# One 512-column matmul in place of two pieces of 264 and 248 in the projections of a two-block network on Trainium2

## The chip, the cores and the metric

The kernel runs on one core of one Trainium2 chip. The metric is the device time of one execution in microseconds (us). Three runs of the kernel before gave 1912.60, 1915.05 and 1916.12 us, a median of 1915.05 us.

## What is computed

One sequence of 512 tokens with 1024 features goes through two blocks, all in float32.

```
for l in range(2):                         # block 1, over 528 rows: 16 meta tokens + 512
    a, g, zc, q, k, v, za, qi, ki, wi = split(h @ w_in[l])
    y_conv = silu(layer_norm(conv31(a * sigmoid(g)))) * silu(zc)
    y_attn = attention(q, k, v, keys = top 132 by relu(qi.ki)*wi) * silu(za)
    h = layer_norm(alpha * h + [y_conv, y_attn] @ w_out[l])
# block 2, over the 512 tokens
proj = rmsnorm(h) @ w_in_2                 # windowed attention, gated linear attention, gates
merged = sigmoid(g_att) * (attn @ w_branch_attn) + sigmoid(g_gla) * (gla @ w_branch_gla)
h = h + merged @ w_out_2
h = h + expert_choice_ffn(rmsnorm(h))      # 16 experts, 64 tokens each
h = h + sigmoid(rmsnorm(h) @ w_ple_gate) * (p @ w_ple);  out = rmsnorm(h)
```

## The kernel before, in words

**Projections.** Nearly all products of activations with weights go through `proj` (L166 to L183). The result is feature-major: 128 output features on the partitions, tokens along the columns. The 1024 input features are eight tiles of 128 (`KT`). Weights and activations are each split in a high and a low part of type float32r (`wh`, `wl`; `hTh`, `hTl` or `xTh`, `xTl`), and three products per tile are added up in PSUM: high by high, high weight by low activation, low weight by high activation. One output tile is thus 8 x 3 products over all its tokens. In a product the 128 x 128 weights are loaded into TensorE and the activations stream through. `segs` names the tokens: either the two halves (0, 264) and (264, 528) of the 528 rows of block 1, in a PSUM bank each, or a single stretch of 512 tokens, in one bank. A stretch is walked in steps of `self.piece` columns, and each step is one matmul with a weight load of its own:

```
n = segs[0][1] - segs[0][0]
...
k = self.piece or c1 - c0
for x in range(0, n, k):
    nc.tensor.matmul(ps[:m, s, x:min(x + k, n)], a[:, t, :m], b[:, c0 + x:min(c0 + x + k, c1)],
```

**Where 512 tokens are one stretch.** In block 1: the index queries of both layers, and in the second layer also the queries, the two gates and the output projection (activations `hT`, `yah`/`yal`, `ych`/`ycl`). In block 2: every projection (activations `xT`, `at`, `yg`, `mh`/`ml`), among them one with only 48 output features.

**Weights.** `load_w` brings 256 columns of weights from HBM over SyncE's queue (SP); `split_w` makes `wh` on ScalarE (ACT, L159) and `wl` on VectorE (DVE, L160).

**Block 1.** Beside the projections, the convolution has 31 taps for four tiles of 128 channels. A tile's input `u` is made at L325 from two products; some tiles' taps go to ACT and GpSimd (POOL) and the others to DVE, first tap at L313 and thirty at L315. After all four tiles the channel statistics (L641) start the tail of the layer, which ends in the output projection. The selection of keys (L398, L399) and a pass of the softmax of the attention (L568) also run on DVE.

**Block 2 and the experts.** After the projections with their attention and linear attention comes the output projection. Then the weights of the 16 experts stream from HBM through buffers that earlier work leaves free (`rawe`, issued at L1484 and L1489 on SP), and each is multiplied as it arrives (L1505). The end is a gate product (L1587) of 512 columns with 128 x 128 weights of type float32r in each matmul, issued without pieces, and the final norm.

**The order of work.** Instructions are written in streams of different urgency (`levels`, `go`), and a scheduler puts them in an order per engine when the program is built, by urgency and by modelled durations (`schedule_with_timeline_sim=True`). Each engine executes its own list in that order. A change of the matmuls thus also changes where other instructions stand.

Of the kernel before, what the change touches and what calls it, by code (L numbers as in the profile page):

```python
# [16 lines left out]
PSUM = bass.MemoryType.PSUM  # L17
DRAM = bass.MemoryType.DRAM
# [9 lines left out]
TOPK = min(256, L // 4)  # L28
# [5 lines left out]
def constants():  # L34
# [6 lines left out]
    p = np.arange(128)[:, None]  # L41
# [5 lines left out]
    # second block  # L47
# [10 lines left out]
    same = (p // 64) == (c // 64)  # L58
# [10 lines left out]
class Net:  # L69
    def __init__(self, tc, I, out, dbg=None, upto=99):  # L70
        self.tc, self.nc, self.I, self.out, self.dbg = tc, tc.nc, I, out, dbg
        self.upto = upto
        self.bgq = []
        self.plan = [
            (('w', 'topk', 'tail', 'idx', 'proj', 'conv', 'att', 'ag', 'rest', 'fill'),
             ('ag0', 'idx', 'q', 'k', 'sc', 'v', 'ag2', 'ag3', 'topk', 'ag1', 'zc', 'att', 'za'),
             (2, 0, 1, 3),
             (2, 3, 1, 0),
             (0, 1, 2)),
            (('w', 'tail', 'idx', 'conv', 'proj', 'att', 'ag', 'topk', 'rest', 'fill'),  # L80
             ('idx', 'q', 'k', 'sc', 'ag1', 'v', 'ag0', 'ag3', 'topk', 'ag2', 'att', 'za', 'zc'),
             (2, 0, 1, 3),
             (2, 3, 1, 0),
             (0, 1)),
        ]
        self.order2 = ('w', 'crit', 'att', 'gla', 'main', 'late', 'fill')
        self.gn0, self.apull, self.gpull, self.ng = 2, 3, (1, 0, 2, 1), 0
        self.early = ("u", "szc", "cv", "qi", "v", "sm", "sm", "parts", "hw", "hl", "raw", "raw", "raw", "c1")
        self.last = ("raw", "u", "szc", "qi")
        self.cycle = ("u", "szc", "qi", "v", "sm", "sm", "hw", "hl", "raw", "raw", "raw")  # L90
        self.piece = 264
        self.swap = True
        self.stack = True
        self.sqsum, self.sqe, self.xlp = 'v', 'AAAAAAAA', ()
        self.pairs2 = False
        self.pairs, self.spare = False, None
        self.cur = None
        self.pos = 0

    def levels(self, *names):  # L100
        """streams of instructions, the earlier named the more urgent to the scheduler"""
# [11 lines left out]
    def go(self, name):  # L113
        """continue in the stream of that name"""
# [105 lines left out]
    def pair(self, out, k):  # L220
        """keys of two heads on the partitions -> side by side, each on its own half of the partitions"""
# [6 lines left out]
    def halves(self, name, q):  # L228
        """two heads of 64 on the partitions of q [128, x, n] -> high parts of the one beside the low parts of the same"""
# [8 lines left out]
    def dots(self, out, qs, p, x, kh, kl):  # L238
        """products of head (x, p) with keys, whose high parts are on both halves of the partitions"""
# [17 lines left out]
    def layer(self, l):  # L257
# [15 lines left out]
        # per-channel vectors of the convolution, channels on partitions  # L273
# [21 lines left out]
        # convolution input  # L295
# [40 lines left out]
        def p_idx():  # L336
            self.go("idx")
            # index keys and queries
# [18 lines left out]
        # index scores  # L357
# [34 lines left out]
        # selection of the TOPK largest scores of each row, as an additive bias  # L392
# [10 lines left out]
        # the same for rows hardly longer than TOPK: all but the smallest, ties to the lower index  # L403
# [68 lines left out]
        # attention  # L472
# [4 lines left out]
        def gated(col, r, src):  # L477
            """rows of the attention, turned and gated"""
# [146 lines left out]
        # layer norm over the channels of the convolution, tokens on partitions  # L625
# [45 lines left out]
        # output projection, residual and layer norm  # L671
# [70 lines left out]
    def embedding_product(self):  # L742
        """per-layer embedding product, kept in DRAM until the end"""
# [6 lines left out]
        w = []  # L750
# [21 lines left out]
    def rms(self, dst, src, gain):  # L772
        """dst = src / rms(src) * gain, rows on partitions"""
# [8 lines left out]
    def scaled(self, t, ps, raw):  # L782
        """columns times their scale, which a raw product needn't wait for"""
# [4 lines left out]
    def to_tokens(self, ps, evac, raw=False):  # L788
        """feature-major [128, 512] in PSUM -> PSUM [128 tokens, 4, 128]"""
# [48 lines left out]
    def window_attn(self, n):  # L838
        """generator of steps for the query tile n"""
# [192 lines left out]
    def second_block(self):  # L1032
# [29 lines left out]
        # last layer norm's gain and offset, and the rms norm, features on partitions  # L1062
# [38 lines left out]
        # the rows' scale joins after the products  # L1101
# [10 lines left out]
        # windowed attention inputs  # L1112
# [30 lines left out]
        # gated linear attention inputs  # L1143
# [41 lines left out]
        # gated linear attention, with projections in between  # L1185
# [41 lines left out]
        # normalised output, gated  # L1227
# [14 lines left out]
        # merged branches  # L1242
# [17 lines left out]
    def experts(self, mx):  # L1260
# [19 lines left out]
        # output projection, residual, router product and statistics  # L1280
# [44 lines left out]
        # affinities  # L1325
# [32 lines left out]
        # slots on partitions (twice), and indices along the free dimension on every partition  # L1358
# [9 lines left out]
        # expert feed-forward: the weights stream by, two rows of 128 at a time  # L1368
# [106 lines left out]
        def chunk(w, t):  # L1475
            """rows t and t + 1 of the tiles of w, each a list of pieces side by side"""
# [42 lines left out]
        # per-layer embedding gate's weights, split while the last expert is computed  # L1519
# [16 lines left out]
        # per-layer embedding and final norm, a tile of tokens at a time  # L1536
# [14 lines left out]
        def rms4():  # L1551
            """half the reciprocal root mean squares of the rows"""
# [117 lines left out]
```

## Time and profile before

| | |
|---|---|
| three runs | 1912.60, 1915.05, 1916.12 us |
| profiled execution: its time is given as its span | 1904.8 us |
| mean granted TensorE clock | 0.968 |
| PE busy (TensorE matmuls) | 1785.8 us, 94% of the span, 11679 instructions |
| PEld busy (weight loads) | 1404.4 us, 74%, 11679 instructions |
| DVE busy | 1087.8 us, 57% |
| ACT busy | 831.8 us, 44% |
| POOL busy | 226.6 us, 12% |
| HBM read | 302.60 MB |

The span reaches from the first to the last instruction; the runs' median lies 10.2 us above it. Matmuls are pipelined: the duration of one is longer than its distance from the next, so this document takes the price of a matmul from the starts of those that follow each other, and "busy" of PE is the time in which at least one is under way. In the rows, `128*128` are the rows and columns of the weights and `128x264 f32` is the matmul's output.

### The profile page before, as it was taken

What the parts mean: (1) busy time and instruction counts of PE and PEld (TensorE: products, weight loads), DVE (VectorE), ACT (ScalarE), POOL (GpSimd) and SP (SyncE); (2) the same over time, 40 slices, a digit from 0 to 9 for tenths busy, and PEclk for the clock granted to TensorE, in tenths of its full rate; (3) what the DMA queues carried; (4) which work ended last, traced back from release to release, by engine and by line L of the source; (5) the groups of instructions that cost most, each with busy time, mean ns of one, the idle gap of its engine ahead of it and who ended that gap; (6) DMA issues with size and microseconds to landing.
All of it is one profiled execution on the core that took longest, in us unless ns stands there. A gap on an engine that the chain in (4) does not pass through costs nothing.

```text
span 1904.8 us, 28702 instructions
## 1 busy us (share of the span) xinstructions
PE 1785.8 (94%) x11679; PEld 1404.4 (74%) x11679; DVE 1087.8 (57%) x2019; ACT 831.8 (44%) x1384; POOL 226.6 (12%) x154
## 2 busy tenths in 40 slices
PE   6999979889999899799999999999799999999978
PEld 6889868878988799797788899999444544344346
DVE  3889994667799976864443446544422323323254
ACT  4864656456567353633355544323122221221245
POOL 1621863000068300000000000000000000000000
PEclk9999999889999899899999999999899999999989
DMA  5213111122122122222112248456599999999961
GB/s 188 67 45 90 45 45 45 29 69 67 56 58 77 45 67 67 79 86 67 34 45 89 79 139 266 144 200 244 209 381 409 409 409 409 409 409 409 409 253 44
DMA packets 164083, 318.67 MB, mean 167 GB/s; under 512 B 12738, under 2 KB 102522, under 8 KB 163824
## 3 DMA queue, kind: packets, MB, share of 16 engines
q1 hardware_dynamic: 160832, 312.63, 45.3%
q10 hardware_dynamic: 3120, 4.21, 0.7%
q8 instruction: 92, 1.51, 0.3%
q14 instruction: 39, 0.32, 0.0%
HBM read 302.60 MB, written 14.16 MB: 166 GB/s over the span
## 4 chain that ended last, share of the span: by engine, by line
PE 74%; DVE 16%; ACT 5%; issue 3%; DMA 2%; POOL 0%; SPq 0%; ACTq 0%; DVEq 0%; POOLq 0%
PE pp L181 36%; PE pp L1505 17%; DVE cv L315 3%; PE pp L1587 2%; DVE wl L160 2%; PE pgat L1396 2%; PE psc L1449 2%; PE phid L1426 2%; PE pidx L243 1%; PE po L550 1%; DVE acc L399 1%; DVE m L398 1%; PE pidx L242 1%; PE po L889 1%; DMA rawe<-in_w_exp_up 1%
## 5 line engine op out<-in xcount | busy, mean ns | idle before, releaser
L310 POOL TENSOR_TENSOR cv<-cv,prod 128x528 f32<-128x528 f32 (+1 forms) x150 | 226.4, 1509 | 417.5 <-ACT prod L308 409.6
L159 ACT CAST wh<-raw 128x1024 fp32r<-128x1024 f32 (+2 forms) x149 | 151.0, 1016 | 257.6 <-PE pp L181 230.6
L1505 PE MATMUL pp<-rawe,xf 128*64 128x512 f32 x1024 | 246.9, 606 | 2.6 <-DMA rawe<-in_w_exp_up 1.0
L181 PE MATMUL pp<-hTh,wh 128*128 128x264 f32 (+2 forms) x1056 | 226.5, 294 | 13.5 <-ACT th L324 4.9
L160 DVE TENSOR_TENSOR wl<-raw,wh 128x1024 fp32r<-128x1024 f32 (+2 forms) x149 | 188.8, 1267 | 69.3 <-ACT wh L159 60.8
L181 PE MATMUL pp<-hTl,wh 128*128 128x264 f32 (+2 forms) x1056 | 223.6, 292 | 0.0
L181 PE MATMUL pp<-hTh,wl 128*128 128x264 f32 (+2 forms) x1056 | 223.6, 291 | 0.0
L181 PEld LDWEIGHTS pp<-hTh,wh 128*128 128x128 f32 (+1 forms) x1056 | 167.8, 192 | 23.9 <-issue 7.9
L1505 PEld LDWEIGHTS pp<-rawe,xf 128*64 128x64 f32 x1024 | 78.5, 138 | 136.2 <-issue 129.4
L181 PEld LDWEIGHTS pp<-hTl,wh 128*128 128x128 f32 (+1 forms) x1056 | 166.7, 192 | 8.5 <-issue 8.1
L181 PEld LDWEIGHTS pp<-hTh,wl 128*128 128x128 f32 (+1 forms) x1056 | 166.7, 192 | 7.9 <-issue 7.5
L181 PE MATMUL pp<-xTh,wh 128*128 128x264 f32 (+1 forms) x752 | 156.8, 290 | 2.9 <-ACT op L980 2.3
L181 PE MATMUL pp<-xTl,wh 128*128 128x264 f32 (+1 forms) x752 | 158.3, 290 | 0.4 <-DVE xTl L1075 0.4
L181 PE MATMUL pp<-xTh,wl 128*128 128x264 f32 (+1 forms) x752 | 156.4, 288 | 0.0
L308 ACT ACTIVATE prod<-u,taps 128x528 f32<-128x528 f32 (+1 forms) x150 | 107.2, 728 | 42.2 <-POOL cv L310 41.8
L181 PEld LDWEIGHTS pp<-xTh,wh 128*128 128x128 f32 (+1 forms) x752 | 116.7, 190 | 5.6 <-ACT op L980 2.5
L181 PEld LDWEIGHTS pp<-xTl,wh 128*128 128x128 f32 (+1 forms) x752 | 116.5, 190 | 3.6 <-issue 2.6
L1505 PE MATMUL pp<-rawe,hid 128*64 128x512 f32 x512 | 118.7, 593 | 0.2 <-DMA rawe<-in_w_exp_down 0.2
L181 PEld LDWEIGHTS pp<-xTh,wl 128*128 128x128 f32 (+1 forms) x752 | 116.2, 189 | 3.4 <-issue 3.3
L1428 ACT COPY hid<-phid 128x512 f32<-128x512 f32 x16 | 9.4, 586 | 204.6 <-PE phid L1426 181.6
L1505 PEld LDWEIGHTS pp<-rawe,hid 128*64 128x64 f32 x512 | 42.2, 137 | 68.8 <-issue 64.9
L315 DVE SCALAR_TENSOR_TENSOR cv<-u,taps,cv 128x512 f32<-128x512 f32 (+1 forms) x90 | 89.0, 1000 | 0.6
(505 smaller groups left out, 3171.7 us busy)
## 6 DMA issues: line engine op xcount, KB each, us to landing
rawe<-in_w_exp_down SPq DMA_DIRECT2D x54, 1024.0 KB, 15.3
rawe<-in_w_exp_up SPq DMA_DIRECT2D x52, 1024.0 KB, 15.3
rawe<-in_w_exp_gate SPq DMA_DIRECT2D x51, 1024.0 KB, 14.4
raw<-in_w_in SPq DMA_DIRECT2D x45, 1024.0 KB, 5.5
rawe<-in_w_exp_gate SPq DMA_DIRECT2D x26, 512.0 KB, 16.5
rawe<-in_w_exp_up SPq DMA_DIRECT2D x22, 512.0 KB, 16.4
raw<-in_w_in SPq DMA_DIRECT2D x20, 512.0 KB, 4.3
rawe<-in_w_exp_down SPq DMA_DIRECT2D x20, 512.0 KB, 13.0
```

The source lines that it names most:

```text
L159: nc.scalar.copy(wh, raw_view)
L160: nc.vector.tensor_sub(wl, raw_view, wh.bitcast(F32))
L181: nc.tensor.matmul(ps[:m, s, x:min(x + k, n)], a[:, t, :m], b[:, c0 + x:min(c0 + x + k, c1)], start=(t == 0 and pi == 0 and x == 0), stop= ...
L242: nc.tensor.matmul(out, qs[:, p, x, :], kh, start=True, stop=False)
L308: nc.scalar.activation(pr, src, AF.Identity, scale=taps[:, c, j:j + 1], bias=0.0 if j else cvec[:, c, 31:32])
L310: nc.gpsimd.tensor_tensor(cv[:, c, :], cv[:, c, :], pr, op=ALU.add)
L315: nc.vector.scalar_tensor_tensor(cv[:, c, :], src, taps[:, c, j:j + 1], cv[:, c, :], op0=ALU.mult, op1=ALU.add)
L1396: nc.tensor.matmul(ps, oh[:, i, :], (zh, zl)[k][:, s, i, :], start=(i == 0 and k == 0), stop=(i == 3 and k == 1))
L1426: nc.tensor.matmul(ph[:, t, :], ul[:, t * 128:(t + 1) * 128], both, start=True, stop=True)
L1449: nc.tensor.matmul(ps, ohts[j][:, 128 * i:128 * (i + 1)], Ys[j][:, k, s * 512:(s + 1) * 512], start=(k == 0), stop=(k == 1))
L1505: nc.tensor.matmul(ps[64 * k:64 * k + 64, s, :], lhs, r, start=(t == 0), stop=(t == KT - 2), skip_group_check=True)
L1587: nc.tensor.matmul(ps[k][:, k, :], a[:, t, :], wp[t][:, w, k * 512:(k + 1) * 512], start=(t == 0 and pi == 0), stop=(t == KT - 1 and pi == 2))
```

## The change

`self.piece` becomes 512, so that the loop above runs once for a stretch of 512 tokens. Stretches of 264 are as before.

```diff
         self.cycle = ("u", "szc", "qi", "v", "sm", "sm", "hw", "hl", "raw", "raw", "raw")
-        self.piece = 264
+        self.piece = 512
         self.swap = True
```

The rest of the diff blanks comments and docstrings; line numbers stay. In the program, 2280 matmuls of 264 columns and 2280 of 248 columns become 2280 of 512 columns. The matmuls of L181 in stretches of 264 (2592) remain.

The order of the instructions changes with it. On PE in block 2, in the projections of `xT` (`xTh`, `xTl`) between pieces of the windowed attention (`po` and `tp`), there stood before

```order
L181 MATMUL pp<-xTl,wh 128x264
L181 MATMUL pp<-xTl,wh 128x248
L181 MATMUL pp<-xTh,wl 128x264
L181 MATMUL pp<-xTh,wl 128x248
L889 MATMUL po<-pT,v_8051 64x512
L883 MATMUL tp<-base,sm 128x128 x8
L181 MATMUL pp<-xTh,wh 128x264
L181 MATMUL pp<-xTh,wh 128x248
L889 MATMUL po<-pT,v_8051 64x512
```

and now stands

```order
L181 MATMUL pp<-xTh,wh 128x512
L181 MATMUL pp<-xTl,wh 128x512
L889 MATMUL po<-pT,v_7379 64x512
L883 MATMUL tp<-base,sm 128x128 x6
L889 MATMUL po<-pT,v_7379 64x512
L883 MATMUL tp<-base,sm 128x128 x6
L181 MATMUL pp<-xTh,wl 128x512
```

Each pair of pieces is one row now, and the attention's pieces stand closer together here.

On DVE in the second layer of block 1, around the input `u` and the first tap (`cv<-u,taps,cvec`, L313) of the last tile of the convolution that DVE computes, there stood before

```order
L160 TENSOR_TENSOR wl<-raw,wh 128x1024
L325 SCALAR_TENSOR_TENSOR u<-th,pp 128x528
L315 SCALAR_TENSOR_TENSOR cv<-u,taps,cv 128x512
L533 TENSOR_TENSOR smm_6476<-psm,acc 128x128
L313 TENSOR_SCALAR cv<-u,taps,cvec 128x512
L315 SCALAR_TENSOR_TENSOR cv<-u,taps,cv 128x512
L534 TENSOR_REDUCE mi<-smm_6476 128x8
L315 SCALAR_TENSOR_TENSOR cv<-u,taps,cv 128x512 x3
L492 TENSOR_TENSOR yas<-po,rs 128x512
L315 SCALAR_TENSOR_TENSOR cv<-u,taps,cv 128x512 x2
L568 ISA smb,mx<-pidx,acc,mi 128x256
```

and now stands

```order
L568 ISA smb,mx<-pidx,acc,mi 128x256
L568 ISA mx 128x1
L315 SCALAR_TENSOR_TENSOR cv<-u,taps,cv 128x512
L570 TENSOR_SCALAR mx<-mx 128x2
L160 TENSOR_TENSOR wl<-raw,wh 128x1024
L315 SCALAR_TENSOR_TENSOR cv<-u,taps,cv 128x512
L579 SCALAR_TENSOR_TENSOR smm_6188<-smm_6188,mx 128x128
L325 SCALAR_TENSOR_TENSOR u<-th,pp 128x528
L315 SCALAR_TENSOR_TENSOR cv<-u,taps,cv 128x512
L313 TENSOR_SCALAR cv<-u,taps,cvec 128x512
```

The first tap of this tile stood ahead of the eight softmax steps (L568, 128x256) of a query tile, and stands behind them now, with six more taps of the other tile ahead of it.

A little later on DVE, just ahead of the channel statistics (L641) of the same layer, there stood before

```order
L579 SCALAR_TENSOR_TENSOR smm_6579<-smm_6579,mx 128x128
L160 TENSOR_TENSOR wl<-raw,wh 128x1024
L248 SCALAR_TENSOR_TENSOR szc<-th,pp 128x512
L582 TENSOR_REDUCE sx<-smm_6579 128x8
L583 TENSOR_TENSOR ssum<-ssum,sx 128x8
L490 RECIPROCAL rs<-ssum 128x8
L491 TENSOR_SCALAR rs<-rs 128x8
L641 BN_STATS cst<-tp 128x6
```

and now stands

```order
L248 SCALAR_TENSOR_TENSOR szc<-th,pp 128x512
L568 ISA smb,mx<-pidx,acc,mi 128x512
L568 ISA mx 128x1
L570 TENSOR_SCALAR mx<-mx 128x1
L579 SCALAR_TENSOR_TENSOR smm_6291<-smm_6291,mx 128x128
L582 TENSOR_REDUCE sx<-smm_6291 128x8
L583 TENSOR_TENSOR ssum<-ssum,sx 128x8
L490 RECIPROCAL rs<-ssum 128x8
L491 TENSOR_SCALAR rs<-rs 128x8
L160 TENSOR_TENSOR wl<-raw,wh 128x1024
L248 SCALAR_TENSOR_TENSOR szc<-th,pp 128x512
L641 BN_STATS cst<-tp 128x6
```

One more weight split (L160) with its gate (L248) stands ahead of L641 now. On ACT rows move in the same places; on SP four stores and loads of intermediate results of block 2 move by one place, and no load of weights does; POOL's list is the same.

## Rows read from the trace of the kernel before

**Rows 1.** Chain of waits of the whole span, by engine and by line.

```profile
PE 74%; DVE 16%; ACT 5%; issue 3%; DMA 2%; POOL 0%; SPq 0%; ACTq 0%; DVEq 0%; POOLq 0%
```

**Rows 2.** Stretches: busy us of each engine (instructions), granted clock, DMA share, GB/s.

```profile
600.00:692.00 92.00, 82.86 (x581) 71.81 (x579) 89.11 (x163) 44.05 (x97) 32.88 (x21) 0.94 0.14 47
...
800.00:1340.00 540.00, 528.68 (x3929) 478.48 (x3927) 268.20 (x474) 222.60 (x379) 0.00 (x0) 1.00 0.38 126
1340.00:1800.00 460.00, 441.28 (x2066) 203.71 (x2068) 137.06 (x196) 95.60 (x105) 0.00 (x0) 0.97 0.98 388
```

**Rows 3.** Who waited for whom, SyncE's DMA queue after 1100 us: total, times, longest.

```profile
SPq L1484 <- PE pp L1505: 169.8, 89, 22.1
```

**Rows 4.** Groups by line and shape on PE: count, busy us, mean ns, idle before.

```profile
L181 PE MATMUL pp<-xTh,wh 128*128 128x248 f32 x368 | 104.7, 285 | 0.0
L181 PE MATMUL pp<-hTh,wh 128*128 128x248 f32 x160 | 46.0, 287 | 0.0
L181 PE MATMUL pp<-yg,wh 128*128 128x248 f32 x128 | 32.7, 276 | 0.0
```

**Rows 5.** Timeline of PE, projection of xT: start us, merged length us; 53 rows.

```profile
877.95 0.40 PE L181 MATMUL pp<-xTh,wh 128*128 128x264 f32 x2
...
890.43 0.40 PE L181 MATMUL pp<-xTl,wh 128*128 128x264 f32 x2
```

**Rows 6.** Timeline of PE, projection of hT in block 1; 11 rows.

```profile
438.33 0.40 PE L181 MATMUL pp<-hTh,wl 128*128 128x264 f32 x2
...
440.69 0.40 PE L181 MATMUL pp<-hTh,wh 128*128 128x264 f32 x2
```

**Rows 7.** Chain of waits in order of time, the gate product at the end.

```profile
1855.49 15.34 PE pp L1587 x66
1871.70 24.38 PE pp L1587 x105
```

**Rows 8.** Timeline of PE, the quickest stretch of the same product.

```profile
1862.57 1.08 PE L1587 MATMUL pp<-wp,xh 128*128 128x512 f32 x4
1863.48 0.62 PE L1587 MATMUL pp<-wp,xl 128*128 128x512 f32 x2
1863.94 1.07 PE L1587 MATMUL pp<-wp,xh 128*128 128x512 f32 x4
```

**Rows 9.** Timeline of PE, a 512-column matmul ahead of one with 64-row weights.

```profile
102.47 0.39 PE L242 MATMUL pidx<-kih,qis 128*128 128x512 f32 x1
102.79 0.49 PE L243 MATMUL pidx<-kil,qis 64*128 64x512 f32 x1
```

**Rows 10.** Chain of waits, matmuls of 128 columns with 128 x 128 weights.

```profile
1320.60 6.12 PE pp L766 x54
```

**Rows 11.** Groups of DVE by line: count, busy us, mean ns, idle before and releaser.

```profile
L315 DVE SCALAR_TENSOR_TENSOR cv<-u,taps,cv 128x512 f32<-128x512 f32 (+1 forms) x90 | 89.0, 1000 | 0.6
...
L568 DVE CUSTOM_DVE_ANT_0 smb<-pidx,acc,mi 128x384 f32<-128x384 f32 (+3 forms) x64 | 32.7, 539 | 11.1 <-PE pidx L562 11.1
...
L568 DVE DVE_READ_ACCUMULATOR2_ANT mx<- 128x1 f32 x64 | 4.9, 77 | 0.0
```

**Rows 12.** Timeline of DVE at the end of the second layer's convolution.

```profile
696.40 1.22 DVE L160 TENSOR_TENSOR wl<-raw,wh 128x1024 fp32r<-128x1024 f32 x1 [3.87 <-ACT wh L159]
697.54 0.68 DVE L248 SCALAR_TENSOR_TENSOR szc<-th,pp 128x512 f32<-128x512 f32 x1
...
700.96 0.70 DVE L641 BATCH_NORM_STATS2 cst<-tp 128x6 f32<-128x512 f32 x1 [1.90 <-ACT xct L640]
```

## The prediction

> **What bounds the kernel now.** I read the chain of waits first: 74% of the span is TensorE's work and 16% DVE's [rows 1]. The busy times by stretch then say where that holds [rows 2]. Between 800 and 1340 us, in block 2, PE is busy for 528.68 of 540 us at clock 1.00 (the 2.4 GHz level), so 2% of the stretch is idle and a matmul that gets shorter shortens the stretch. Between 600 and 692 us, in the second layer of block 1, DVE is busy for 89.11 of 92 us and PE for 82.86: there DVE sets the pace, and what PE saves is not passed on. Between 1340 and 1800 us the transfers are at 0.98 of their share and 388 GB/s: the experts are paced by their weights from HBM. This stream is no fixed end. Its queue waits 169.8 us for PE to free buffers [rows 3], and ahead of it, from 800 to 1340 us, the DMA share is only 0.38 [rows 2]. If block 2 ends earlier, the stream starts earlier and ends earlier by as much.
>
> **What goes and what comes.** The change replaces 2280 pairs of matmuls by 2280 single ones. By activation they are: xT, 3 x 376 = 1128 (the groups show 368 of each of the three products [rows 4], and 8 more of each have 48 output features); at, yg, mh and ml, 480 (the largest group is the 128 of yg [rows 4]); and in block 1, hT with 3 x 160 [rows 4] and the output projection's 192, together 672. With each pair one weight load goes too.
>
> The price is the distance of starts, not the duration. For xT the starts of 53 pairs lie between 877.95 and 890.43 us: 12.48 / 52 = 0.240 us a pair [rows 5]. For hT it is (440.69 - 438.33) / 10 = 0.236 us [rows 6]. I use 236 ns for at, yg, mh and ml as well, being nearest in kind.
>
> The single matmul does not stand in L181 yet, but the gate product at the end has its very shape: 512 columns, 128 x 128 weights of float32r, another load for each. It takes 24.38 / 105 = 232.2 ns and 15.34 / 66 = 232.4 ns [rows 7]. I take 232.2. Its quickest stretch has six in 1.37 us, 228.3 ns [rows 8]: the lower bound. The upper bound is a load that isn't hidden: ahead of a matmul with 64-row weights a 512-column matmul is 320 ns from the next [rows 9]. I take the value of rows 7, because there as in `proj` each 128-row load follows another; the 320 ns stays as a rival.
>
> So a pair saves 7.8 ns for xT and 3.8 ns elsewhere. That is small because the pieces were nearly as quick per column as the whole: the load of a piece is hidden already. Where a matmul has only 128 columns, they are 6.12 / 54 = 113 ns apart [rows 10], and both pieces stand above this floor, at 118 to 120 ns on average.
>
> **On the path.** Block 2: 1128 x 7.8 ns = 8.8 us, and 480 x 3.8 ns = 1.8 us; of these 10.6 us I count 98%, the busy share of the stretch [rows 2]: 10.4 us. Block 1: 672 x 3.8 ns = 2.6 us. About 0.6 of it counts, 1.5 us, by my choice: the index queries and the output projection wait for little, while the gates and queries lie where DVE sets the pace. PE thus gives 11.9 us.
>
> **The order.** The scheduler has moved rows on PE, ACT and DVE. On PE the number of products is the same, and what stands between them too; I cost it at nothing, since in block 2 the lists of DVE and ACT have slack (268.20 and 222.60 us busy of 540 [rows 2]). If that cover were gone, PE would wait for one more split, 1.22 us, each time. On DVE in the second layer one more split and gate stand ahead of the channel statistics: 1.22 + 0.68 = 1.9 us [rows 12]. As DVE is full there, I count 1.9 us of loss. The softmax steps that now stand ahead of the last tile's first tap are work that stood ahead of the statistics before too, so they cost nothing as long as DVE isn't left waiting; the rivals price the opposite. SP's four moves are among stores and reloads that are used much later, and cost nothing while the reload lands before its use. No wait is added.
>
> The sum is 1.9 - 11.9 = -10.0 us: 1894.8 us of span against the profiled 1904.8. The runs' median is 10.2 us above this span, and I take that distance as kept: 1915.05 - 10.0 = **1905.0 us**.
>
> **A rule against the row.** The row says that the wide matmul costs 232.2 ns, and that a pair of xT costs 240. The Trainium skill's page "TensorE: Matmul & The Clock Gate" (section "Back-to-back issue gap") gives N / 2.4 + 2.5 ns for a warm matmul, so 215.8 ns for 512 columns and 112.5 + 105.8 = 218.3 for the pieces. The trace doesn't agree with either figure, being 16 and 18 to 22 ns above them; by that rule a pair would save the fixed part alone, 2.5 ns. It is the third rival.
>
> **Rivals.**
> - *The wide matmul is slower in the xT stage.* A pair there costs 4 ns more than one of hT (240 against 236), and I don't know why. If the cause stays with the wide matmul, it costs 236 and saves 3.8 everywhere: 1608 x 3.8 x 0.98 = 6.0, with 1.5 and -1.9 a gain of 5.6 us, 1909.4 us.
> - *Order in the second layer eats the gain.* The last tile's first tap stands behind eight softmax steps of 0.539 + 0.077 us and six taps of 1.000 us: 10.9 us of DVE work [rows 11]. If the end of the convolution slips by it all, 1915.05 - 11.9 + 10.9 = 1914.1 us: no change. For it speaks that DVE is 97% busy there; against it, that the sum of DVE's work is the same.
> - *Only the fixed part is saved.* With 2.5 ns a pair: 1608 x 2.5 x 0.98 = 3.9, and 672 x 2.5 x 0.6 = 1.0, less 1.9: a gain of 3.0 us, 1912.0 us. Rows 7 speak against it.
> - *Slower: DVE waits where it now stands.* The softmax step waits for PE's scores (11.1 us in all [rows 11]). Ahead of the last tile these waits come when DVE has nothing else: its list is in order, and behind the waiting step stand the weight split that PE needs next, the gate and all taps of the last tile. Then the slip is 10.9 + 11.1 = 22.0 us, and the time 1915.05 - 11.9 + 22.0 = 1925.2 us. It decides if the statistics slip by over 15.7 us (11.9 and 3.8), beyond 717 us against 700.96 [rows 12].
> - *Slower by the load.* If the load isn't hidden, each wide matmul costs 320 instead of 232 ns; 7% of the 2280 would eat the gain (0.07 x 2280 x 88 ns = 14 us). The 171 matmuls of rows 7 average 232, so none of it shows there. I leave it 2 in 100, outside the range.
>
> **How the numbers follow.** A measurement of this kernel can tell some 0.2%, or 3.8 us, from no change: faster is below 1911.2, slower above 1918.9. The forecast has 0.50, the slower xT stage 0.17, the order that eats the gain 0.13, the fixed part alone 0.06, DVE's waits 0.12 and the load 0.02. The first two are faster: 0.67. The third and fourth are no change: 0.19. The last two are slower: 0.14. The forecast's own range is 1897 to 1910: at 228.3 ns a pair saves 3.9 more, and with the same shares (1608 x 0.98 + 672 x 0.6 = 1979) that is 7.7 us. The full range goes from 1895, with the 1.9 us of order not lost on top of that, to 1921, past the case of no change and towards the slower one at 1925.2, which with the load is left half out.
>
> **What would show it.** The profile after should have 2280 matmuls and loads less each, 128x512 rows of L181 that start 0.232 us apart (0.236 would be the first rival, 0.240 no gain), and PEld far less busy. Block 2's projections should shrink by some 10 us, the first expert matmul and the end of the weight stream come as much earlier, at the same GB/s. L641 of the second layer should start within 2 us of 700.96; past 712 the order has eaten the gain, past 717 the sign is wrong. The forecast is wrong if wide matmuls are over 0.240 us apart, or if PE's idle time in block 2 grows by what its work shrinks.

## The result and the profile after

The changed kernel takes **1933.41 us** (median of 4 runs, 1933.18 to 1935.19) beside 1914.13 us of the kernel before on the same chip (1912.60 to 1916.12): a ratio of **1.0103 [1.0089, 1.0118]**, so it is slower by about 19 us. Its profiled execution has a span of 1933.4 us. A time is 1.8 us above its span (1935.19 us beside 1933.4), so the profiled execution of the kernel before took some 1906.6 us by estimate, 7.5 less than the median of its runs, and that of the changed kernel is 1.8 above its median: of the 28.6 us between the two spans 19.3 are the change's. The page of the changed kernel gives, for the engines' busy time and the chain of waits by engine [rows 1]:

```profile
PE 1785.3 (92%) x9399; PEld 1289.8 (67%) x9399; DVE 1081.8 (56%) x2019; ACT 834.3 (43%) x1384; POOL 224.0 (12%) x154
...
PE 70%; DVE 13%; ACT 6%; DMA 6%; issue 3%; POOL 2%; ACTq 0%; DVEq 0%; POOLq 0%; SPq 0%
```

The 2280 matmuls and loads are gone (11679 before, 9399 now). PE's busy time is still what it was, though the matmuls are cheaper: in experiment e1 below, the same matmuls in the old order, it is 1772.5 us, at a mean granted clock of 0.968 where the changed kernel has 0.959. The chain of waits doesn't show the loss. What it holds less of PE, 70% where it was 74%, is at L1505, the expert products (13% where they were 17%), where transfers of weights now stand in the chain; L181 has 36% in both, and the chain of the quick e1 holds 6% of DMA as well.

**The single matmul has the price that was forecast.** On the groups by line and shape the counts of [rows 4] return with 512 columns, each where a pair was:

```profile
L181 PE MATMUL pp<-xTh,wh 128*128 128x512 f32 x368 | 149.6, 408 | 5.2 <-ACT op L980 3.1 <-DVE tt L786 1.5 <-DVE th L1251 0.3
...
L181 PE MATMUL pp<-hTh,wh 128*128 128x512 f32 x160 | 66.0, 413 | 2.4 <-DVE kiT L216 1.7 <-ACT th L324 0.8
...
L181 PE MATMUL pp<-yg,wh 128*128 128x512 f32 x128 | 41.4, 398 | 0.5 <-ACT yg L195 0.4 <-DVE th L1222 0.2
```

The distance is again read from the timeline of PE. In the projection of `xT` 34 matmuls follow each other, and in that of `hT` 17 (compare [rows 5, 6]; the first and the last row are shown):

```profile
904.03 0.39 PE L181 MATMUL pp<-xTl,wh 128*128 128x512 f32 x1
...
911.70 0.40 PE L181 MATMUL pp<-xTl,wh 128*128 128x512 f32 x1
```

```profile
440.21 0.40 PE L181 MATMUL pp<-hTh,wl 128*128 128x512 f32 x1
...
443.95 0.40 PE L181 MATMUL pp<-hTh,wh 128*128 128x512 f32 x1
```

That is 7.67 / 33 = 232.4 ns and 3.74 / 16 = 233.8 ns, against 240 and 236 for the pairs.

**The stretches.** The first two lines are the stretches of [rows 2], the third is the experts' stretch 30 us later, as they start later:

```profile
600.00:692.00 92.00, 81.76 (x448) 65.64 (x448) 81.48 (x153) 43.63 (x95) 32.44 (x22) 0.90 0.15 46
...
800.00:1340.00 540.00, 513.93 (x2246) 387.58 (x2245) 262.24 (x445) 223.56 (x378) 0.00 (x0) 0.97 0.35 114
...
1370.00:1830.00 460.00, 440.44 (x2078) 202.00 (x2079) 136.30 (x194) 95.61 (x105) 0.00 (x0) 0.98 0.98 388
```

Three things are to be seen. The experts run as before, 388 GB/s at a DMA share of 0.98, only shifted: from the first expert product to the end it is 547.6 us before and 546.7 after. Their queue waits less for PE [rows 3]:

```profile
SPq L1484 <- PE pp L1505: 150.1, 79, 22.5
```

In the second layer DVE, which was busy for 89.11 of 92 us, is now busy for 81.48. And in block 2 PE stands for 26 of 540 us where it stood for 11, at a mean clock of 0.97 instead of 1.00.

**Where the 28.6 us of span went.** The table gives the start of an instruction in each trace, in us. The last four columns belong to the experiments below.

| | before | after | all lists as before (e1) | PE's list as before (e5) | attention of block 2 as before (e8) | rest of second layer as before (e9) |
|---|---|---|---|---|---|---|
| L325, `u` of the third tile, second layer | 602.2 | 613.5 | 602.5 | 596.6 | 614.2 | 611.9 |
| L641, last of the second layer | 705.7 | 722.6 | 705.6 | 701.6 | 723.0 | 709.7 |
| L1068, first of block 2 | 771.5 | 788.7 | 770.8 | 766.7 | 788.6 | 775.2 |
| L917, first of the linear attention | 979.2 | 1005.3 | 973.3 | 972.7 | 991.8 | 993.6 |
| L1236, last, end of the linear attention | 1192.1 | 1223.2 | 1183.4 | 1182.3 | 1205.1 | 1211.3 |
| L1505, first expert product | 1357.2 | 1386.7 | 1345.0 | 1343.9 | 1367.3 | 1374.9 |
| span | 1904.8 | 1933.4 | 1893.9 | 1892.4 | 1913.5 | 1921.7 |

Before to after, 17 us are lost at the end of the second layer's convolution, and another 14 between L1068 and L1236, in a stretch where e1, with the same matmuls in the old order, gains 8.0. The 17 us repeat: the last L641 starts between 722.3 and 723.0 in the traces of e2, e8 and e11 below, which have the new order there, and at 705.6 in e1.

**The second layer, row by row.** The timeline of DVE shows the place of the forecast's order argument, here around the third tile of the convolution in the changed kernel:

```profile
605.28 0.69 DVE L492 TENSOR_TENSOR yas<-po,rs 128x512 f32<-128x512 f32 x1 [4.75 <-PE po L591]
...
611.53 2.05 DVE L160 TENSOR_TENSOR wl<-raw,wh 128x1024 fp32r<-128x1024 f32 x1 [0.23 <-ACT wh L159]
613.50 0.69 DVE L325 SCALAR_TENSOR_TENSOR u<-th,pp 128x528 f32<-128x528 f32 x1
614.23 0.55 DVE L313 TENSOR_SCALAR cv<-u,taps,cvec 128x512 f32<-128x512 f32 x1
```

and that of ACT what L160 and L325 wait for:

```profile
608.48 0.73 ACT L308 ACTIVATE prod<-u,taps 128x512 f32<-128x512 f32 x1 [0.65 <-POOL cv L310]
609.84 0.72 ACT L308 ACTIVATE prod<-u,taps 128x512 f32<-128x512 f32 x1 [0.63 <-POOL cv L310]
610.47 1.03 ACT L159 CAST wh<-raw 128x1024 fp32r<-128x1024 f32 x1
611.40 0.60 ACT L324 ACTIVATE th<-pp 128x528 f32<-128x528 f32 x1
```

DVE stands idle for 4.75 us until PE has done the attention's output (L591): in its list L492 now stands ahead of the split (L160) and of `u`, where before it came behind `u` (at 602.79, `u` at 602.18). ACT's L324, which needs the products of the tile, and L159, which PE needs for the next weights, stand behind taps that are paced by GpSimd's additions, one every 1.36 us. The rows show why the third tile is late; how much of the 17 us hangs on each of these waits is asked of e7 and e9 below. Further on DVE waits 2.75 us for ACT at L582, where it had no such wait before, and 5.20 at L160 (3.87 before [rows 12]). The last L641 starts at 722.64, 17 us later than before:

```profile
704.63 0.29 DVE L582 TENSOR_REDUCE sx<-smm 128x8 f32<-128x128 f32 x1 [2.75 <-ACT smm L580]
...
710.77 1.23 DVE L160 TENSOR_TENSOR wl<-raw,wh 128x1024 fp32r<-128x1024 f32 x1 [5.20 <-ACT wh L159]
...
714.74 0.70 DVE L641 BATCH_NORM_STATS2 cst<-tp 128x6 f32<-128x512 f32 x1 [2.15 <-ACT xct L640]
...
722.64 0.69 DVE L641 BATCH_NORM_STATS2 cst<-tp 128x6 f32<-128x512 f32 x1
```

In the kernel before, the last one is

```profile
705.75 0.70 DVE L641 BATCH_NORM_STATS2 cst<-tp 128x6 f32<-128x512 f32 x1 [0.81 <-ACT xct L640]
```

The stretches from 594 us to the last L641, before and after (the third number after the length is DVE's busy time), say how much DVE stood idle:

```profile
594.00:706.00 112.00, 102.69 (x743) 90.88 (x743) 99.98 (x187) 56.78 (x121) 37.39 (x25) 0.95 0.13 43
```

```profile
594.00:723.00 129.00, 115.13 (x643) 93.19 (x641) 103.95 (x197) 62.24 (x128) 35.07 (x25) 0.92 0.17 53
```

That is 12.0 us before and 25.0 after: 13 of the 17 us are idle time of DVE.

**Block 2, row by row.** PE's list in the changed kernel, from the last window attention (L883, L889) to the linear attention (L917, L928, L953), reads:

```
L181 MATMUL pp<-xTh,wl 128x512
L883 MATMUL tp<-base,sm 128x128 x8
L795 MATMUL tp<-base,tt 128x128 x4
L889 MATMUL po<-pT,v_7379 64x512
...
L917 MATMUL pl<-up,zT 128x512 x2
L795 MATMUL tp<-base,tt 128x128 x4
L181 MATMUL pp<-at,wh 128x512 x2
...
L928 MATMUL pb<-c_7206,la 128x128 x4
L953 MATMUL pk<-base,ket 128x128 x4
```

(One L889, L917 or L928 of the list is two rows in the trace.) Between L917 and L928 stand 12 products, between L928 and L953 none. Before, 22 products of 512 tokens stood between L917 and L928, and 23 between L928 and L953. From PE's L928 the way to L953 leads over ACT (L930, L932) and DVE (L935 to L949), and PE now has nothing to do meanwhile. In the kernel before, PE's rows there have no wait:

```profile
987.32 1.05 PE L928 MATMUL pb<-c,la 128*128 128x128 f32 x8
...
993.89 0.61 PE L953 MATMUL pk<-base,ket 128*128 128x128 f32 x4
```

From the end of L928 to L953 it is 5.52 us, filled with products. After, it is 6.11 us of waiting. The timeline of PE and the stretches (of 14 and 10 us; the number behind POOL is the granted clock) show the price:

```profile
1012.32 1.05 PE L928 MATMUL pb<-c,la 128*128 128x128 f32 x8
1019.48 1.11 PE L953 MATMUL pk<-base,ket 128*128 128x128 f32 x4 [6.11 <-DVE ket L949]
```

```profile
1005.00:1019.00 14.00, 7.34 (x29) 5.11 (x28) 5.22 (x10) 11.72 (x17) 0.00 (x0) 0.84 0.10 27
1019.00:1029.00 10.00, 9.52 (x36) 7.71 (x37) 3.18 (x9) 2.77 (x5) 0.00 (x0) 0.54 0.15 42
```

PE stands for nearly half of the first stretch, and in the second it works mostly at the 1.2 GHz level. Over the whole of block 2's attention, from L1107 to the last L1236, the stretches give before, after, and in e8 and e5:

```profile
800.00:1192.00 392.00, 385.56 (x2738) 339.59 (x2737) 191.76 (x334) 176.75 (x317) 0.00 (x0) 1.00 0.31 99
```

```profile
819.00:1223.00 404.00, 381.90 (x1675) 283.52 (x1674) 188.64 (x329) 177.82 (x317) 0.00 (x0) 0.97 0.30 96
```

```profile
817.00:1205.00 388.00, 378.53 (x1683) 279.24 (x1682) 190.21 (x332) 177.69 (x317) 0.00 (x0) 1.00 0.32 100
```

```profile
795.00:1182.00 387.00, 380.32 (x1682) 281.13 (x1681) 191.57 (x335) 177.46 (x318) 0.00 (x0) 0.99 0.32 100
```

PE's idle time is the length less its busy time: 6.4 us before, 22.1 after, 9.5 and 6.7 in the two experiments. The wait of 6.1 us at L953 is thus the largest part of what came in, but not the whole. In the changed kernel PE also waits 2.8 us for DVE at L883 and 1.5 at L181 (for L786) in the window attention, and 1.0 at L795 (for L786) behind L917; the kernel before has none of these.

### The profile page after: what moved, and what is told of

Its sections match the earlier page's. It is cut to its first block, busy times and chain, and to the rows that moved or that the text cites. A ratio compares the mean times of both kernels' runs of the same rounds, so it can differ in the third digit from the quotient of the medians.

```text
span 1933.4 us, 24147 instructions
## 1 busy us (share of the span) xinstructions
PE 1785.3 (92%) x9399; PEld 1289.8 (67%) x9399; DVE 1081.8 (56%) x2019; ACT 834.3 (43%) x1384; POOL 224.0 (12%) x154
## 4 chain that ended last, share of the span: by engine, by line
PE 70%; DVE 13%; ACT 6%; DMA 6%; issue 3%; POOL 2%; ACTq 0%; DVEq 0%; POOLq 0%; SPq 0%
PE pp L181 36%; PE pp L1505 13%; DVE cv L315 2%; PE pp L1587 2%; PE pgat L1396 2%; DMA rawe<-in_w_exp_down 2%; DMA rawe<-in_w_exp_gate 2%; DVE wl L160 2%; POOL cv L310 2%; PE psc L1449 1%; PE pidx L243 1%; PE phid L1426 1%; PE pidx L242 1%; PE po L550 1%; PE po L889 1%
## 5 line engine op out<-in xcount | busy, mean ns | idle before, releaser
L159 ACT CAST wh<-raw 128x1024 fp32r<-128x1024 f32 (+2 forms) x149 | 151.0, 1016 | 299.2 <-PE pp L181 267.6
L1505 PE MATMUL pp<-rawe,xf 128*64 128x512 f32 x1024 | 243.9, 599 | 4.2 <-DMA rawe<-in_w_exp_up 2.3
L181 PE MATMUL pp<-hTh,wh 128*128 128x264 f32 (+2 forms) x896 | 226.8, 319 | 14.6 <-ACT th L324 7.7
L181 PE MATMUL pp<-hTl,wh 128*128 128x264 f32 (+2 forms) x896 | 227.8, 319 | 0.0
L160 DVE TENSOR_TENSOR wl<-raw,wh 128x1024 fp32r<-128x1024 f32 (+2 forms) x149 | 186.6, 1253 | 72.7 <-ACT wh L159 70.8
L181 PE MATMUL pp<-hTh,wl 128*128 128x264 f32 (+2 forms) x896 | 223.2, 316 | 0.0
L181 PEld LDWEIGHTS pp<-hTh,wh 128*128 128x128 f32 (+1 forms) x896 | 150.9, 196 | 33.3 <-issue 9.7
L1505 PEld LDWEIGHTS pp<-rawe,xf 128*64 128x64 f32 x1024 | 77.5, 137 | 136.5 <-issue 127.4
L181 PEld LDWEIGHTS pp<-hTl,wh 128*128 128x128 f32 (+1 forms) x896 | 151.4, 195 | 15.4 <-issue 8.4
L181 PEld LDWEIGHTS pp<-hTh,wl 128*128 128x128 f32 (+1 forms) x896 | 150.3, 195 | 13.1 <-issue 6.3
L181 PE MATMUL pp<-xTh,wh 128*128 128x512 f32 (+1 forms) x376 | 152.8, 408 | 5.2 <-ACT op L980 3.1
L181 PE MATMUL pp<-xTl,wh 128*128 128x512 f32 (+1 forms) x376 | 150.3, 400 | 0.8 <-DVE xTl L1075 0.8
L181 PE MATMUL pp<-xTh,wl 128*128 128x512 f32 (+1 forms) x376 | 150.3, 400 | 0.0
L1505 PE MATMUL pp<-rawe,hid 128*64 128x512 f32 x512 | 119.6, 595 | 2.6 <-DMA rawe<-in_w_exp_down 2.5
L1505 PEld LDWEIGHTS pp<-rawe,hid 128*64 128x64 f32 x512 | 41.9, 137 | 72.8 <-issue 62.6
L181 PEld LDWEIGHTS pp<-xTh,wh 128*128 128x128 f32 (+1 forms) x376 | 71.1, 189 | 25.0 <-ACT op L980 3.5
L181 PEld LDWEIGHTS pp<-xTl,wh 128*128 128x128 f32 (+1 forms) x376 | 70.9, 189 | 18.9 <-issue 1.3
L181 PEld LDWEIGHTS pp<-xTh,wl 128*128 128x128 f32 (+1 forms) x376 | 70.8, 188 | 17.2 <-issue 0.4
```

Source lines behind the costliest of these rows:

```text
L159: nc.scalar.copy(wh, raw_view)
L160: nc.vector.tensor_sub(wl, raw_view, wh.bitcast(F32))
L1505: nc.tensor.matmul(ps[64 * k:64 * k + 64, s, :], lhs, r, start=(t == 0), stop=(t == KT - 2), skip_group_check=True)
```

## The experiments

Two theories stood at the start. A: the wide matmul brings the gain that was forecast, and the order of the lists that came with it costs more. B: the wide matmul itself holds others up (loads, PSUM, the engines that wait for a whole stretch), whatever the order. One edit, used in many runs, tells them apart: a table of numbers holds engines to a chosen order, by dependencies without a semaphore between neighbours of a list. It adds no instruction that computes and no wait of one engine for another.

```diff
+ORDER = {"PE": ..., "DVE": ..., "ACT": ..., "SP": ...}
+
+def keep_order(tc, nc):
...
+        for a, b in zip(order[:-1], order[1:]):
+            tc.add_manual_dep(mine[b], mine[a].name, mybir.DependencyInfo(mybir.DependencyClass.NoSync, mybir.DependencyReason.DATA), reason="order")
...
                 self.second_block()
+            keep_order(tc, self.nc)
```

**e1: wide matmuls, all four lists in the order of before** (a pair's place is taken by its single matmul).

> The wide matmuls of the change, with the instructions of PE, DVE, ACT and SP held to the order of the kernel before (a wide matmul stands where the second piece of its pair stood). Theory A, the new order costs the time and the wide matmul gains: about 1902 us (1914 less the 10 to 12 us of the forecast's sum), block 2 again without idle time. Theory B, the wide matmul itself holds the other engines up (a coarser grain, less chance to slip work between): 1925 us or more, whatever the order.

Measured: 1898.37 us (5 runs), ratio 0.9929 [0.9902, 0.9956], a gain of 13.6 us. By spans it is 11.0 us (1904.8 to 1893.9). L641 is at 705.6 as before, and the gain builds up where it was forecast: 0.7 us by L1068, 8.7 by L1236, 12.2 by the first expert product.

**e2: pieces of 264 and 248 as before, all four lists in the order of the changed kernel.**

> The two pieces of the kernel before, with all four engines held to the order of the changed kernel (both pieces stand where the wide matmul stood). Theory A: slower than the changed kernel, by the 10 to 12 us that the wide matmul gains where PE sets the pace, less what lies in idle time: 1936 to 1946 us, and the idle time of PE in block 2 as in the changed kernel. Theory B: the time of the kernel before, about 1914 us.

Measured: 1945.62 us (4 runs), ratio 1.0177 [1.0150, 1.0204]. The order alone costs 1.77% of 1912 us, 34 us. Within the intervals the two effects add up: on the order of before the wide matmul gives 0.71%, on the new order (1.0103 / 1.0177) 0.73%. The waits of PE in block 2 show that the pieces suffer as the wide matmuls do; L953 leads the list with 7.3 us, where the changed kernel has 6.1. B falls.

**e3 and e4: the wide matmul in one block only, with the scheduler's own order for each.** In e3 `self.piece` stays 264 for block 1, in e4 for block 2. The edit of e3 is shown; e4 has 264 at the same place of the changed kernel:

```diff
             if self.upto > 1:
+                self.piece = 512
                 self.second_block()
```

> Wide matmuls in block 2 alone, pieces in block 1, the order made by the scheduler. Theory A: block 1 is as before (its statistics L641 near 701 us), so the 17 us lost there are gone; block 2 loses its 12 us if the scheduler gives it the order of the changed kernel there: about 1926 us, or about 1904 if the order comes out another way. Theory B: the 12 us of block 2 and no more, 1926 us.

> Wide matmuls in block 1 alone, pieces in block 2, the order made by the scheduler. Theory A: the loss of block 1, 17 us at the end of its second layer, is there as in the changed kernel, and block 2 keeps its idle-free stretch: about 1931 us. Theory B says the same; the two differ in the other runs.

Measured: e3 1925.80 us, ratio 1.0078 [1.0056, 1.0100]; e4 1924.77 us, ratio 1.0066 [1.0041, 1.0092]. In e3 the second layer ends near where it did: block 1 has the lists of before, and the 4.1 us by which L641 is later (709.8) arise in the first 140 us of that execution. Block 2 loses 14.3 us between L1068 and L1236, with 7.3 us at L953, and the time is the 1926 us expected. In e4 L641 starts at 723.3 and L1068 17.8 us late, and hardly anything is lost behind; the time is 6 us below the 1931 expected. So there are two separate losses, and either of them eats more than the whole gain. The two ratios add up to 28 us, above the 20 of the change; each has an interval of 4 to 5 us to either side.

**e5 and e6: which engine's list.** In e5 only PE's list is held to the order of before, in e6 only DVE's and ACT's; the matmuls are wide in both.

```diff
-ORDER = {"PE": ..., "DVE": ..., "ACT": ..., "SP": ...}
+ORDER = {"PE": ...}
```

> Only PE's list is held to the order of before (wide matmuls); DVE, ACT and SP are left to the scheduler, which moves no DVE row by more than 9 places. Theory P, PE's list carries the loss: close to the run with all four lists held, 1898 us (ratio 0.993 to before), last channel statistics (L641) of the second layer near 706 us, first L1303 near 1264. Theory D, the lists of DVE and ACT carry it: over 1915 us, L641 past 715. I expect P.

> The reverse: DVE's and ACT's lists are held to the order of before, PE's is left to the scheduler (rows up to 59 places from before). Theory P: PE's own list brings part of the loss back, 1910 to 1930 us, with waits of PE in block 2 of 10 us or more. Theory D: near 1898 us with PE's waits in block 2 as before (some 6 us). I expect in between and nearer to D, about 1903 us, because PE's list follows the order in which splits come out of DVE.

Measured: e5 **1894.75 us** (4 runs), ratio **0.9911 [0.9894, 0.9927]**: with PE's list held, all of it comes back, and the version beats both kernels. e6 1939.60 us, ratio 1.0145 [1.0128, 1.0162], no better than the changed kernel; I had expected 1903. The waits of PE in block 2 stand there at other places, led by

```profile
PE tp L795 <- DVE tt L786: 7.4, 2, 5.8
PE pp L181 <- ACT op L980: 5.1, 2, 2.8
PE pp L181 <- DVE es L870: 2.6, 1, 2.6
```

while in e5 the list is that of the kernel before:

```profile
PE pp L181 <- ACT op L980: 4.7, 2, 2.3
PE pp L976 <- DVE A L970: 0.8, 1, 0.8
```

So the old order of DVE and ACT does not help beside a new one of PE, and given PE's old list the scheduler makes good ones for the others. That PE's list alone carries the loss isn't shown by this: the DVE list that the scheduler made in e5 is close to that of before, and no run has PE's old list beside the changed kernel's lists of DVE and ACT.

**e7: the first part of the second layer's stretch as before.** The order of the changed kernel, with 216 rows of PE, 41 of DVE and 23 of ACT put back.

> The order of the changed kernel everywhere except for one stretch of the second layer (41 DVE rows, 23 ACT rows, 216 PE rows, as before): there the weight split of the fourth convolution tile (L160) stands again ahead of the attention's softmax end and of the split of its output (L490 to L492), instead of behind it. What comes after, eight softmax steps ahead of u (L325) of the third tile, stays as in the changed kernel. Theory S, the split behind the attention starts the slip: u of the third tile goes from 613.5 back to about 604 us, the last L641 from 722.6 to about 712, and the time from 1933 to about 1923 us. Theory T, the softmax steps ahead of u and the first taps make it: u stays past 610, L641 near 722, time within 4 us of 1933.

Measured: 1938.95 us (4 runs), ratio 1.0131 [1.0111, 1.0151]. The split stands ahead again, DVE now waits there 5.5 us for ACT's L159, and `u` still starts at 614.9, the last L641 even at 727.4. Theory S falls; the time is 5.5 us above 1933, past the 4 us that theory T allowed.

**e8: the window attention of block 2 as before.** PE from L1107 to the first L928, DVE and ACT beside it; all else as in the changed kernel.

> The order of the changed kernel everywhere except for the window attention of block 2 (PE from L1107 to the first L928, DVE and ACT beside it), which has the order of before: its scores stand again between the products of the keys, queries and values (L1163, L1167) and not behind them. The linear attention behind it keeps the order of the changed kernel from its first L953 on. The second layer of block 1 is as in the changed kernel, so 17 us stay lost there. Theory C, the weights' products run ahead and are missing as cover when the linear attention starts: L917 at about 992 instead of 1005 us, PE's wait of 6 us at L953 under 2, time about 1918 us. Theory G, the linear attention's own order costs it: L917 near 1000, the wait at L953 remains, time over 1927 us.

Measured: 1915.14 us (12 runs), ratio 1.0024 [1.0008, 1.0040], about the expected 1918: by the ratios, 15 of the order's 33 us (1.0103 - 0.9929) come back. L917 starts at 991.8 (expected 992), and between L928 and L953 stand 23 products again, though from L953 on the linear attention keeps the new order. The wait at L953 is gone from the list of PE's waits in block 2, which begins

```profile
PE pp L181 <- ACT op L980: 4.6, 2, 2.3
PE pp L976 <- DVE A L970: 1.6, 2, 0.8
```

Theory C holds: where the products of the weights stand between the steps of the attention, PE's work covers their waits. Done ahead, they are missing later.

**e9: the rest of the second layer's stretch as before**, from where e7 ended to the output projection.

> The order of the changed kernel everywhere except for the second part of the second layer's stretch (PE rows from the fourth tile's products to the output projection, DVE and ACT beside them), which is as before; the first part, which the last run but one put back without effect, is as in the changed kernel. Theory T, the loss of block 1 arises where the attention's products stand ahead of the convolution tiles' products in PE's list and seven taps (L308) stand ahead of L159 and L324 in ACT's: the last L641 goes from 722.6 back to about 708, the time from 1933 to about 1919 us, with block 2's loss kept. Rival U, the stretch only goes wrong as a whole (either part in the new order loses it all): L641 stays near 722, time within 4 us of 1933.

Measured: 1922.70 us (9 runs), ratio 1.0051 [1.0034, 1.0067]. The last L641 starts at

```profile
709.70 0.70 DVE L641 BATCH_NORM_STATS2 cst<-tp 128x6 f32<-128x512 f32 x1 [0.90 <-ACT xct L640]
```

so 13 of the 17 us are back, about as theory T expected (708), and U falls. By the ratios it is 10 us of the time. DVE's idle time from 594 us on is 16.9 us, against 12.0 before and 25.0 in the changed kernel:

```profile
594.00:710.00 116.00, 104.20 (x614) 84.03 (x613) 99.10 (x191) 58.67 (x125) 35.89 (x24) 0.94 0.16 50
```

The 13 us don't hang on DVE's wait for PE at L492. It is still there, and `u` of the third tile still starts at 611.9, while ACT's L159 and L324 stand 9 us earlier than in the changed kernel, nearly where they were before (599.1 and 600.0):

```profile
605.67 0.69 DVE L492 TENSOR_TENSOR yas<-po,rs 128x512 f32<-128x512 f32 x1 [5.43 <-PE po L591]
```

```profile
601.37 1.05 ACT L159 CAST wh<-raw 128x1024 fp32r<-128x1024 f32 x1
602.32 0.61 ACT L324 ACTIVATE th<-pp 128x528 f32<-128x528 f32 x1
```

Which of this stretch's rows on PE, DVE and ACT brings the time back is not told apart by this run.

**e10: PE's list of the changed kernel with these two stretches as before**; DVE, ACT and SP left to the scheduler.

> PE's list of the changed kernel, with only two stretches of it put back to the order of before: the second part of the second layer (575 rows) and block 2's window attention (744 rows); DVE, ACT and SP are left to the scheduler. If these two stretches of PE's list carry the loss (theory P, located): 1895 to 1900 us as with PE's whole list held, L641 near 706, L1303 near 1266. If the rest of PE's list or the lists of DVE and ACT matter as well: over 1910 us.

Measured: 1907.99 us (12 runs), ratio 0.9974 [0.9960, 0.9989]. It lies between the two expectations. 1319 rows of PE turn the sign, and of the 37 us between the changed kernel and e5 (1.0103 - 0.9911 = 1.92%) they bring 25. The last L641 starts at 709.5, where e9 has 709.7 with the rows of DVE and ACT put back too: in the second layer PE's rows are enough, with the lists that the scheduler makes for the others. L1068 is at 775.0 where e5 has 766.7, and L1303 13 us later than there: the rest lies in both blocks, in rows that I did not follow.

**e11: 24 products moved.** Of the changed kernel's order, the 24 products of L1199 that stand ahead of the last L883 go behind L917 and L928, with 12 of L1204; two weight splits that reuse their buffers move along.

> The order of the changed kernel with one small move: the 24 products of the gate weights (L1199) that PE does ahead of the last scores of the window attention (L883) stand behind the first product of the linear attention (13 behind L917, 11 behind L928, with the 12 of L1204 behind these), and the two weight splits that reuse their buffers go behind L949 on DVE and L932 on ACT. Theory C, cover is missing there: PE's wait at L953 for DVE's L949 goes from 6.1 to under 1 us, the first L963 from 1020.4 to about 1015, the time from 1933 to about 1928 us. Rival: the wait moves to the next step (L917, or the second L953) and the time stays within 2 us of 1933.

Measured: 1927.47 us (7 runs), ratio 1.0073 [1.0052, 1.0093]. The median is 6 us lower, as expected, but the interval touches that of the changed kernel, and the execution that the rows are from has a span of 1933.9 us. In it, the wait at L953 shrank from 6.1 to 1.5 us (under 1 was expected), and another grew from 2.8 us to

```profile
PE tp L883 <- DVE sm L876: 6.2, 3, 3.4
...
PE pk L953 <- DVE ket L949: 1.5, 1, 1.5
```

The first L963 starts at 1020.4 as in the changed kernel, not at 1015. So the cover can be moved by hand to the wait, and is then missing at the place it was taken from; whether anything is won stays open.

**e12: another cut, 256 and 256.** In block 1's stretches of 264 nothing changes.

```diff
-                    k = self.piece or c1 - c0
+                    k = 256 if n == 512 else 264
```

> As before, but with 512 columns in two pieces of 256 and 256 instead of 264 and 248; the scheduler's own order, which moves 1044 of 10157 PE rows by at most 28 places and 382 DVE rows by at most 9 (the change moves rows by up to 113 and 24). Theory C, only the order of the attention's steps against the weights' products matters, and it is kept here: within 5 us of before, 1908 to 1918 us, L641 of the second layer near 706, L917 near 979, no wait at L953. Rival, any small change of the order costs this kernel tens of us: over 1922 us. A pair of 256 columns should take 236 to 240 ns, as the pair of 264 and 248 does.

Measured: 1901.25 us (5 runs), ratio 0.9946 [0.9933, 0.9960], below the expected 1908 to 1918. The order holds: L641 at 705.4, L917 at 976.6, no wait at L953. A pair costs less than expected. From the timeline of PE, 13 and 43 pairs:

```profile
437.73 0.39 PE L181 MATMUL pp<-hTh,wl 128*128 128x256 f32 x2
...
440.53 0.40 PE L181 MATMUL pp<-hTh,wl 128*128 128x256 f32 x2
```

```profile
878.25 0.40 PE L181 MATMUL pp<-xTl,wh 128*128 128x256 f32 x2
...
888.22 0.40 PE L181 MATMUL pp<-xTl,wh 128*128 128x256 f32 x2
```

2.80 / 12 = 233.3 ns and 9.97 / 42 = 237.4 ns, where 264 and 248 take 236 and 240. Over 1152 and 1128 pairs that is 1152 x 2.7 + 1128 x 2.6 = 6.0 us, and the span is 5.4 us shorter (1899.4). The medians differ by 11; the profiled execution of the kernel before lies some 6 us below its median of this comparison (1906.6 by the estimate above, 1912.23), which is about the rest. That the price alone makes the gain isn't shown, since the order has moved a little too.

## Why the prediction was wrong

- **What goes and what comes: right.** The single matmul costs 232 to 234 ns in the two stretches read, and 2280 pairs became 2280 matmuls. A pair of xT saves 7.6 ns (7.8 forecast), one of hT 2.2 (3.8 forecast). "PE thus gives 11.9 us" is what e1 shows with the order held: 11.0 us by spans, 13.6 by the ratio. Block 2 was right in kind too: 11.4 us less from L1068 to the first expert product, against 10.4 forecast up to 1340 us.
- **The order: this step failed.** "On PE the number of products is the same, and what stands between them too; I cost it at nothing, since in block 2 the lists of DVE and ACT have slack." e2 shows 34 us for the order alone, and e5 that holding PE's list brings them back. The number of products was the same, but not what stands between them. The slack of DVE and ACT was the wrong measure: from the end of PE's L928 to that of DVE's L949 it is 5.1 us before and 6.1 after, though DVE and ACT are busy for half of block 2 or less. What hides this chain is PE's own products between its two ends, and the number of these was what had changed: from 23 to none. e8 puts them back and the wait is gone. The bound of "one more split, 1.22 us, each time" was taken from the wrong work; that one wait is 6.11 us, and PE's idle time in block 2's attention grew by 15.7.
- **The second layer: the place was right, the price and the cause were not.** The loss of "one more split and gate" was put at 1.9 us. The last L641 slipped by 17 us. The statement that the softmax steps "cost nothing as long as DVE isn't left waiting" names the condition: DVE was left waiting, 13 us more than before from 594 us on, for PE (4.75 us at L492) and for ACT. e9 brings 13 us of the slip back with the wait at L492 still there, so that wait isn't the cause by itself; which rows of the stretch are stays open.
- **Rivals.** The first (236 ns in the xT stage) and the load that isn't hidden fall with the price, and so does the third (only 2.5 ns a pair) for xT; in hT the saving is near it. The second and the fourth put the slip of L641 at 10.9 and 22.0 us; the first L641 slipped by 13.8, the last by 17. The fourth has the right sign, by waits of DVE. It also has no loss in block 2, so that its 1925.2 us fell short by 8. Its threshold was set on the first L641, which stayed at 714.7, below 717, while the tail of the layer starts from the last. And its waits were to be those of the softmax for PE's scores, which have hardly changed, 10.7 us in all where they were 11.1 [rows 11]:

```profile
L568 DVE CUSTOM_DVE_ANT_0 smb<-pidx,acc,mi 128x384 f32<-128x384 f32 (+3 forms) x64 | 33.0, 542 | 10.7 <-PE pidx L562 10.5
```

- **The range** ended at 1921; the rivals priced a loss by the order in the second layer alone. About half of the loss came from where the largest gain was expected. The text's own test was right: the forecast fails "if PE's idle time in block 2 grows by what its work shrinks"; it grew from 6.4 to 22.1 us.

## What to carry to other kernels

Where a scheduler orders the lists from modelled durations, a change of an instruction's shape is two changes: its price, which can be read from like rows, and a new order, which here cost two to three times as much with the opposite sign (34 us beside 11.0 to 13.6). Ahead of a dependent step, count the independent products that the matrix engine's list has between the step and what it waits for, before and after; slack of the other engines did not tell here. If the price is good and the time is not, hold that engine's list to the old order and leave the others to the scheduler: here this turned 1.0103 into 0.9911.

## What the runs showed of the hardware

- Where a stretch is cut matters a little. In hT and xT 256 and 256 columns take 233.3 and 237.4 ns, 264 and 248 take 236 and 240, and 512 in one 233.8 and 232.4: with a load of 128 x 128 float32r weights each, cutting a stretch costs 0 to 5 ns when it is cut in the middle, and some 2.6 more when it is cut at 264.
- The Trainium skill's page "TensorE: Matmul & The Clock Gate" (section "Back-to-back issue gap") gives some 131 ns as a sustained spacing for 512 columns and N / 2.4 + 2.5 as that of single ones, 215.8 ns for 512. The trace agrees with neither here: the 33 distances average 232.4 ns, at a granted clock of 1.00.
- A wait of PE can cost more than itself. After the stretch in which PE was busy for 7.34 of 14 us the granted clock is 0.54 for the next 10. In block 2's attention, PE's busy time for the same work is 381.9 us in the changed kernel, at a mean clock of 0.97, and 378.5 in e8, where it is 1.00.
